# Full-width products, overwritten at once, in front of the compressed scores and of the combination products of an attention layer

## The chip, the cores and the metric

One core of a Trainium2 chip runs one launch of the kernel. The metric is the device time of that launch in microseconds (us). All work is in float32. Matrix products run on TensorE (PE in the profile, with its weight loads as PEld), elementwise work on VectorE (DVE), ScalarE (ACT) and GpSimd (POOL), and SyncE (SP) issues the DMAs. TensorE writes into PSUM, which has eight banks of 128 partitions by 512 float32 columns. The profile also lists the clock that TensorE was granted: 1.00 stands for 2.4 GHz, 0.50 for 1.2 GHz.

## What is computed

Two layers over 512 tokens of width 1024. Each layer is a gated feed-forward network, a mixer, and a second feed-forward network, each with a norm before and after and a residual. The mixer of the first layer is sparse attention (the change lies there), that of the second layer is a recurrent RWKV-7 block. Of the attention, cut to what matters:

```
q, kc, vc, ks, vs, kw, vw, gl = split(u @ w_in)        # 16 query heads, 4 key/value heads
k_cmp = compress(kc); v_cmp = compress(vc)             # 31 compressed blocks of 32 tokens
s_c = q . k_cmp - slope * dist;  p_c = masked softmax; o_c = p_c . v_cmp
s_s = q . ks    - slope * dist;  p_s = masked softmax; o_s = p_s . vs      # selected branch
s_w = q . kw    - slope * dist;  p_w = masked softmax; o_w = p_w . vw      # window branch
out = (g0 * o_c + g1 * o_s + g2 * o_w) @ w_out
```

With 512 tokens all eight selection blocks are taken, so the selected branch and the window branch both are causal attention over all tokens, with keys and values of their own.

## The kernel before

`nsa` first projects the compressed keys and values and the first queries, and then goes through the four key/value groups `g`, each with four query heads `u`, and in each group through the four blocks `b` of 128 queries. For one block `scores` makes q.k for both branches into a bank of PSUM (lines 654 and 655, key parts `kh` and `kl`), VectorE adds the bias and takes the minimum (line 657), ScalarE takes the exponential (line 659). `outputs` turns the weights with transposes (line 671), splits them into two parts (lines 200 and 201), and multiplies them with the values (lines 676 and 678).

Beside these rounds runs a list of other work, `fill`, whose steps are put between theirs by numbers (`BASE`, `PACE`): the remaining projections through `mm3` (line 195, three products for one), and for each group `compressed(g)` and `turned(g)`. `compressed(g)` writes 16 narrow products, one for each block and head (line 601: 128 rows of weights `q`, 32 moving columns of `kcmp`), into the columns of one PSUM bank; VectorE and ScalarE make the softmax from it (lines 604 to 619). The profile shows two records for each of these products. `turned(g)` transposes the result (line 626).

`combine(g-1)` runs inside the first block of group g, and `combine(3)` at the end. It transposes the reciprocal sums (line 698) and then, for each of two pairs of heads `j`, makes the compressed branch's output `cm` (line 706: `vbd`, `pcts`, 64 rows, 512 columns, two records each), spreads the gates with `pick` (line 714), and adds the three branches on VectorE and GpSimd (lines 715 to 717). Behind the attention comes the projection by `w_out` (line 195, `part` and `whi`).

The order of instructions on each engine is not the order of the code: a scheduler with a model of the times sorts them. A scheduler's choice can thus move other work when instructions are added. `xh` is the normed input of the attention, in 8 tiles of 128 features by 512 tokens; it is in place before the attention begins and stays until after it.

Of the kernel before, what the change touches and what calls it, by code (L numbers as in the profile page):

```python
# [16 lines left out]
P = 128  # L17
# [5 lines left out]
NB = S // P  # L23
# [46 lines left out]
class Net:  # L70
# [367 lines left out]
    def nsa(self, xh, xl):  # L438
        nc, io = self.nc, self.io
# [155 lines left out]

        def compressed(g):
            gv = gates[:, :, 12 * g:12 * g + 12].rearrange("p b (u r) -> p b r u", r=3)
            sb = self.bank().rearrange("p (b u n) -> p b u n", b=NB, u=4)
            for b in range(NB):
                for u in range(4):  # L600
                    nc.tensor.matmul(sb[:, b, u, :], qs[4 * g + u][:, b * P:b * P + P].bitcast(F32), kcmp[:, g, :],
                                     start=True, stop=True)
            sc = self.small([P, NB, 4, 32], "scc", 2)
            for u in range(4):
                nc.vector.scalar_tensor_tensor(sc[:, :, u, :], distc, slopes[4 * g + u], sb[:, :, u, :],
                                               op0=OP.mult, op1=OP.add)

            def wide(t):
                return t.rearrange("p b (u o) -> p b u o", o=1).to_broadcast([P, NB, 4, 32])
            mn = self.small([P, NB, 4], "mnc", 2)  # L610
            nc.vector.tensor_reduce(mn, sc, axis=AX.X, op=OP.min)
            nc.vector.tensor_tensor(sc, sc, wide(mn), op=OP.subtract)
            nc.scalar.activation(sc, sc, AF.Exp, scale=-1.0)
            al = self.small([P, NB, 4], "alc", 2)
            nc.vector.tensor_reduce(al, sc, axis=AX.X, op=OP.add)
            nc.vector.reciprocal(al, al)
            nc.vector.tensor_tensor(al, al, gv[:, :, 0, :], op=OP.mult)
            nc.vector.tensor_tensor(sc, sc, wide(al), op=OP.mult)
            nc.vector.tensor_tensor(sc[:, 0], sc[:, 0], maskc, op=OP.mult)
            scs[g] = sc  # L620
            yield
# [42 lines left out]
        def outputs(g, b, brs):  # L664
            tb = slice(b * P, b * P + P)
            for br in brs:
                ac = self.bank("ac")
                for k in range(b + 1):
                    tp = self.bank("pt")
                    for u in range(4):  # L670
                        nc.tensor.transpose(tp[:, u * P:u * P + P], ps[g, b, br, u][:, k * P:k * P + P], self.ident)
                    pt = [self.small([P, S], "pt", NPT, F32R) for _ in range(2)]
                    self.split(tp, *pt)

                    w = vt[k][:, br, g]
                    nc.tensor.matmul(ac, w.rearrange("p i d -> p (i d)"), pt[0], start=k == 0, stop=k == b,
                                     skip_group_check=True)
                    nc.tensor.matmul(ac[0:64], w[:, 0], pt[1], start=False, stop=k == b, skip_group_check=True)
                    yield
                if b + br == 0:  # L680
                    if g:
                        yield from combine(g - 1)
                    os[g] = self.small([P, 2, 2, S], "o", 1)
                hv = self.small([64, S], "hv", 1)
                nc.scalar.activation(hv, ac[64:128], AF.Copy)
                for e in range(2):
                    x, y = [t.rearrange("p (j e t) -> p j e t", j=2, e=2)[:, :, e, :] for t in (ac[0:64], hv)]
                    nc.vector.tensor_add(os[g][64 * e:64 * e + 64, br, :, tb], x, y)

        def combine(g):  # L690
            al, o = als[g % 2], os[g]
            av = al[:, :, 0:8].rearrange("p b (r u) -> p b r u", r=2)
            gv = gates[:, :, 12 * g:12 * g + 12].rearrange("p b (u r) -> p b r u", r=3)
            nc.vector.reciprocal(av, sums[g])
            nc.vector.tensor_tensor(av, av, gv[:, :, 1:3, :], op=OP.mult)
            tp = self.bank("pt")
            for b in range(NB):
                nc.tensor.transpose(tp[0:32, b * P:b * P + P], al[:, b, :], self.ident)
            at = self.small([64, S], "at", 1, F32R)
            nc.scalar.activation(at[0:32], tp[0:32], AF.Copy)  # L700
            nc.vector.tensor_sub(at[32:64], tp[0:32], at[0:32].bitcast(F32))
            yield
            for j in range(2):
                cm = self.bank("pt")
                rows = slice(64 * j, 64 * j + 64)
                nc.tensor.matmul(cm, vbd[g][rows, :], pcts[g][rows, :], start=True, stop=True)
                if len(opair) == KT // 2 and g >= G // 2:

                    t = self.act.tile([P, KT, S], F32, tag="xl", name="xl")
                    opair.extend(t[:, i, :] for i in range(KT // 2))  # L710
                y = opair[2 * g + j]
                for br, dst in ((0, y), (1, o[:, 1, j])):
                    bc = self.bank("sc")
                    nc.tensor.matmul(bc, pick[:, 2 * br + j, :], at, start=True, stop=True)
                    nc.vector.tensor_mul(dst, o[:, br, j], bc)
                nc.vector.tensor_add(y, y, cm)
                nc.gpsimd.tensor_add(y, y, o[:, 1, j])
                yield
# [5 lines left out]
        def all_of(g):  # L724
            for _ in g:
# [8 lines left out]

        bias, sums, ps, os = {}, {}, {}, {}
        fill = Fill(vproj(), gproj(), compressed(0), qproj(2), turned(0), qproj(3), compressed(1), kproj(1, 0), turned(1),
                    kproj(1, 1), qproj(4), qproj(5), compressed(2), qproj(6), turned(2), qproj(7), compressed(3), turned(3))
        rounds = [(g, b, items, brs) for g in range(G) for b in range(NB) for items, brs in ITEMS[b]]
        all_of(scores(*rounds[0][0:3]))
        n = 0  # L740
        for r, (g, b, _, brs) in enumerate(rounds):
            ahead, m = iter(()), 0
            if r + 1 < len(rounds):
                f, c, items, _ = rounds[r + 1]
                if f > g:
# [3 lines left out]
                    n = 0  # L749
# [11 lines left out]
            all_of(ahead)  # L761
        fill.until(1000)
        all_of(combine(G - 1))
        self.kinds = KINDS
        self.pop(2)
# [832 lines left out]
```

## Time and profile before

| | us |
|---|---|
| median of 3 runs (2302.13 to 2304.86) | 2302.98 |
| the profiled execution | 2306.49 |
| its span, first to last instruction | 2304.6 |
| PE busy in the span | 2190.6 (95%) |
| DVE busy | 1527.2 (66%) |
| ACT busy | 1159.3 (50%) |
| mean granted TensorE clock | 0.963 |

The attention's rounds lie from about 447 to 730 us of the span. The page gives the whole execution; what a stage is worth is read from windows cut out of it, where the busy time of each engine stands beside the granted clock. In the timeline a matmul's start is exact and its end is modelled, with neighbours overlapping; the price of one in a row is therefore the time from its start to the start of the next.

### The profile page before, as it was taken

How to read it: one execution, taken by the hardware profiler on the slowest of the kernel's cores; microseconds unless marked ns; L12 is line 12 of the kernel's file. 1: busy time of each engine (PE TensorE's matmuls, PEld its weight loads, DVE VectorE, ACT ScalarE, POOL GpSimd, SP SyncE). 2: the span in 40 equal slices, each digit the busy share in tenths (PEclk: the TensorE clock that was granted, in tenths of full speed). 3: DMA queues.
4: the chain of work that ended last, by engine and by line, in shares of the span. 5: the costliest groups of instructions: out<-in, count | busy, mean ns of one | idle time of the engine just before them, and what ended most of it. 6: DMA issues, size and time to landing. Idle time of an engine off the chain costs nothing.

```text
span 2304.6 us, 38449 instructions
## 1 busy us (share of the span) xinstructions
PE 2190.6 (95%) x15398; PEld 1921.0 (83%) x15398; DVE 1527.2 (66%) x2447; ACT 1159.3 (50%) x2282; POOL 363.9 (16%) x372
## 2 busy tenths in 40 slices
PE   7999999999999999999999999988699989899998
PEld 7999888877666889998799998866587867899987
DVE  8888625346777688872588874386663556888733
ACT  5555514465665455552445554286333754555532
POOL 4000004023100310000130000012493423100000
PEclk9999999999989999999999999999798989999999
DMA  4333333211001323333323333232443124333331
GB/s 174 101 104 111 101 95 109 83 46 46 29 1 65 101 83 110 107 94 102 110 83 100 103 101 108 85 104 92 75 114 122 47 83 162 94 109 99 96 107 67
DMA packets 93283, 214.33 MB, mean 93 GB/s; under 512 B 40752, under 2 KB 41392, under 8 KB 93104
## 3 DMA queue, kind: packets, MB, share of 16 engines
q1 hardware_dynamic: 93104, 211.88, 29.6%
q8 instruction: 121, 1.98, 0.4%
q14 instruction: 58, 0.48, 0.1%
HBM read 196.84 MB, written 15.01 MB: 92 GB/s over the span
## 4 chain that ended last, share of the span: by engine, by line
issue 29%; PE 24%; DVE 5%; POOL 4%; ACT 3%; DMA 1%; SPq 0%; DVEq 0%; POOLq 0%; ACTq 0%
PE p L195 19%; POOL two L1045 1%; POOL tmpi L1043 1%; PE p L1154 1%; ACT junk L218 1%; POOL sp L347 1%; PE p L1178 0%; DVE slot L201 0%; PE p L1170 0%; DVE xl L201 0%; DVE h L261 0%; PE p L972 0%; PE p L862 0%; PE p L1206 0%; PE p L1199 0%
## 5 line engine op out<-in xcount | busy, mean ns | idle before, releaser
L195 PE MATMUL p<-xh,whi 128*128 128x256 f32 (+1 forms) x1640 | 479.4, 296 | 18.3 <-ACT xh L200 8.4
L195 PE MATMUL p<-xl,whi 128*128 128x256 f32 (+1 forms) x1640 | 477.4, 294 | 3.4 <-DVE xl L201 3.4
L195 PE MATMUL p<-xh,wlo 128*128 128x256 f32 (+1 forms) x1640 | 457.9, 294 | 1.4 <-DVE wlo L201 1.4
L174 DVE TENSOR_TENSOR wlo<-raw,whi 128x1024 fp32r<-128x1024 f32 x150 | 190.2, 1269 | 316.7 <-ACT whi L170 316.7
L195 PE MATMUL p<-whi,slot 128*128 128x512 f32 x1280 | 395.1, 389 | 0.0
L195 PE MATMUL p<-slot,whi 128*128 128x256 f32 x1920 | 361.1, 284 | 12.5 <-issue 6.0
L170 ACT ACTIVATE whi<-raw 128x1024 fp32r<-128x1024 f32 x166 | 174.8, 1056 | 339.8 <-PE p L195 314.9
L195 PEld LDWEIGHTS p<-xh,whi 128*128 128x128 f32 x1640 | 319.1, 195 | 29.2 <-ACT xh L200 9.8
L195 PEld LDWEIGHTS p<-xl,whi 128*128 128x128 f32 x1640 | 320.2, 195 | 9.0 <-DVE xl L201 4.7
L195 PEld LDWEIGHTS p<-slot,whi 128*128 128x128 f32 x1920 | 303.4, 193 | 14.9 <-issue 6.2
L195 PEld LDWEIGHTS p<-xh,wlo 128*128 128x128 f32 x1640 | 309.5, 195 | 6.8 <-DVE wlo L201 1.6
L200 ACT ACTIVATE whi<-xn 128x1024 fp32r<-128x1024 f32 (+1 forms) x240 | 220.0, 917 | 184.7 <-PE p L195 133.8
L201 DVE TENSOR_TENSOR wlo<-xn,whi 128x1024 fp32r<-128x1024 f32 (+1 forms) x240 | 255.8, 1067 | 50.1 <-ACT whi L200 47.0
L195 PEld LDWEIGHTS p<-whi,slot 128*128 128x128 f32 x1280 | 240.0, 188 | 49.7
L195 PE MATMUL p<-slot,wlo 128*128 128x256 f32 x960 | 270.1, 284 | 0.0
L195 PE MATMUL p<-wlo,slot 128*128 128x512 f32 x640 | 249.0, 389 | 0.0
L222 POOL TENSOR_TENSOR rstd<-rstd,mhalf 128x1 f32<-128x1 f32 x48 | 30.1, 628 | 1348.0 <-DVE rstd L221 1347.2
L195 PEld LDWEIGHTS p<-slot,wlo 128*128 128x128 f32 x960 | 184.5, 193 | 0.0
L391 ACT ACTIVATE sp<-p 128x256 f32<-128x256 f32 x320 | 121.2, 379 | 112.6 <-PE p L195 112.6
L195 PEld LDWEIGHTS p<-wlo,slot 128*128 128x128 f32 x640 | 120.1, 188 | 24.9
L195 PE MATMUL p<-big,whi 128*128 128x512 f32 (+1 forms) x288 | 94.9, 412 | 12.0 <-ACT big L839 11.2
L200 ACT ACTIVATE whi<-raw 128x1024 fp32r<-128x1024 f32 x80 | 84.1, 1051 | 40.1 <-PE p L195 40.1
(321 smaller groups left out, 3754.1 us busy)
## 6 DMA issues: line engine op xcount, KB each, us to landing
raw<-in_wpack SPq DMA_DIRECT2D x252, 512.0 KB, 3.6
xn<-in_wpack SPq DMA_DIRECT2D x80, 512.0 KB, 3.5
hpark<-h SPq DMA_DIRECT2D x8, 512.0 KB, 2.7
h<-hpark SPq DMA_DIRECT2D x8, 512.0 KB, 4.7
h<-in_x SPq DMA_DIRECT2D x4, 512.0 KB, 7.1
gpost<-in_ffn_norm_post SPq DMA_DIRECT2D x4, 512.0 KB, 6.6
md<-tb SPq DMA_DIRECT2D x8, 256.0 KB, 2.8
td<-two SPq DMA_DIRECT2D x4, 512.0 KB, 2.8
```

The source lines that it names most:

```text
L170: self.last_hi = nc.scalar.activation(hi, raw, AF.Copy)
L174: (eng or nc.vector).tensor_sub(lo, raw, hi.bitcast(F32))
L195: m = self.nc.tensor.matmul(out, lhs[a], rhs[b], start=start and i == 0, stop=stop and i == 2, skip_group_check=more)
L200: i = self.nc.scalar.activation(hi, src, AF.Copy)
L201: return i, (eng or self.nc.vector).tensor_sub(lo, src, hi.bitcast(F32))
L218: nc.scalar.activation(self.junk(), src[q], AF.Square, scale=1.0 / (half * math.sqrt(D)), accum_out=ss[:, q:q + 1])
L222: nc.gpsimd.tensor_tensor(r[:, 1:2], r[:, 0:1], self.mhalf[:, 0:1], op=OP.pow)
L347: nc.gpsimd.tensor_sub(t4, q(xh, 1, 0, b), t2)
L391: copy = lambda dst, bank: nc.scalar.activation(dst, bank[:, 0:H], AF.Copy)
L1043: nc.gpsimd.tensor_tensor(t, ms[:, j, j + 1:32].rearrange("p (i o) -> p i o", o=1).to_broadcast([P, n, m]), T[:, j:j + 1, 0:m].to_broadcas ...
L1045: nc.gpsimd.tensor_tensor(T[:, j + 1:32, 0:m], T[:, j + 1:32, 0:m], t, op=OP.subtract)
L1154: nc.tensor.matmul(gb[e][:, j * P:j * P + P], B[own[e], j, c, :], A[own[e], j, c, :], start=True, stop=True)
```

## The change

In `compressed(g)`, ahead of the four narrow products of each block `b`, one product of `xh` with itself goes into the same bank, over all columns from that block on (512, 384, 256 and 128 columns for b = 0 to 3). In `combine(g)`, ahead of the product into `cm`, two products of 512 columns go into the same bank, for each `j`. All have 128 rows of weights and are written with start=True; the products behind them overwrite what they wrote, so no value of the output depends on them. They come to 16 products in `compressed` and 16 in `combine`, 20 of them with 512 columns.

```diff
         def compressed(g):
             gv = gates[:, :, 12 * g:12 * g + 12].rearrange("p b (u r) -> p b r u", r=3)
-            sb = self.bank().rearrange("p (b u n) -> p b u n", b=NB, u=4)
+            bank = self.bank()
+            sb = bank.rearrange("p (b u n) -> p b u n", b=NB, u=4)
             for b in range(NB):
+
+                nc.tensor.matmul(bank[:, b * P:], xh[:, 0, 0:P], xh[:, 0, b * P:], start=True, stop=True)
                 for u in range(4):
                     nc.tensor.matmul(sb[:, b, u, :], qs[4 * g + u][:, b * P:b * P + P].bitcast(F32), kcmp[:, g, :],
                                      start=True, stop=True)
...
             for j in range(2):
                 cm = self.bank("pt")
                 rows = slice(64 * j, 64 * j + 64)
+                for _ in range(2):
+                    nc.tensor.matmul(cm, xh[:, 0, 0:P], xh[:, 0, :], start=True, stop=True)
                 nc.tensor.matmul(cm, vbd[g][rows, :], pcts[g][rows, :], start=True, stop=True)
```

In the changed file the new products stand on lines 602 and 710; line 601 becomes 604, 654 becomes 657, 655 becomes 658, 671 becomes 674, 676 becomes 679, 678 becomes 681, 698 becomes 701, 706 becomes 711 and 714 becomes 719.

TensorE, the compressed scores of the first group (bank p_5203), before:

```order
L592 MATMUL p_5179<-ident,at 128x64 x4
L601 MATMUL p_5203<-kcmp,q 128x32 x8
L654 MATMUL p_4996<-kh,q 128x384
L655 MATMUL p_4996<-kl,q 128x384
L601 MATMUL p_5203<-kcmp,q 128x32 x2
```

and after:

```order
L592 MATMUL p_5179<-ident,at 128x64 x4
L602 MATMUL p_5203<-xh 128x512
L604 MATMUL p_5203<-kcmp,q 128x32 x4
L602 MATMUL p_5203<-xh 128x384
L604 MATMUL p_5203<-kcmp,q 128x32 x3
L657 MATMUL p_4996<-kh,q 128x384
```

Two of the four new products stand inside what was a row of eight narrow ones; everything ahead of this place on TensorE is unmoved.

TensorE, the compressed scores of the second group (p_5453, after p_5457), before:

```order
L601 MATMUL p_5453<-kcmp,q 128x32 x2
L676 MATMUL p_5122<-pt,vt_3970 128x512
L654 MATMUL p_5408<-kh,q 128x256
L655 MATMUL p_5408<-kl,q 128x256
L601 MATMUL p_5453<-kcmp,q 128x32
L678 MATMUL p_5122<-pt,vt_3970 64x512
```

```order
L601 MATMUL p_5453<-kcmp,q 128x32 x10
L671 MATMUL p_5430<-ident,sp 128x128
L601 MATMUL p_5453<-kcmp,q 128x32 x3
```

and after, where the first combination product of the first group has moved ahead of them:

```order
L710 MATMUL p_5543<-xh 128x512 x2
L711 MATMUL p_5543<-scc,vbd_3981 128x512
L657 MATMUL p_5412<-kh,q 128x256
L658 MATMUL p_5412<-kl,q 128x256
L604 MATMUL p_5457<-kcmp,q 128x32
L602 MATMUL p_5457<-xh 128x384
L604 MATMUL p_5457<-kcmp,q 128x32 x4
L602 MATMUL p_5457<-xh 128x256
L604 MATMUL p_5457<-kcmp,q 128x32 x4
L602 MATMUL p_5457<-xh 128x128
L604 MATMUL p_5457<-kcmp,q 128x32 x3
```

The narrow ones still stand close together, now with three new products among them and two ahead.

TensorE, the compressed scores of the fourth group (p_7081, after p_7105) and the combination of the second (`vbd_3982`), before:

```order
L706 MATMUL p_6251<-scc,vbd_3982 128x512
L654 MATMUL p_6240<-kh,q 128x256
L655 MATMUL p_6240<-kl,q 128x256
L714 MATMUL p_6253<-at,pick 128x512
L671 MATMUL p_6277<-ident,sp 128x128 x4
L601 MATMUL p_7081<-kcmp,q 128x32 x10
L706 MATMUL p_6261<-scc,vbd_3982 128x512
```

and after:

```order
L710 MATMUL p_6267<-xh 128x512 x2
L711 MATMUL p_6267<-scc,vbd_3982 128x512
L657 MATMUL p_6256<-kh,q 128x256
L658 MATMUL p_6256<-kl,q 128x256
L719 MATMUL p_6271<-at,pick 128x512
L674 MATMUL p_6297<-ident,sp 128x128 x4
L604 MATMUL p_7105<-kcmp,q 128x32
L602 MATMUL p_7105<-xh 128x384
L604 MATMUL p_7105<-kcmp,q 128x32 x4
L602 MATMUL p_7105<-xh 128x256
L604 MATMUL p_7105<-kcmp,q 128x32 x4
L710 MATMUL p_6279<-xh 128x512 x2
```

Here the row of ten narrow products is cut by two new ones and stands between two pairs of full width.

## Rows read from the trace of the kernel before

**Rows 1.** The page: engines (busy us, share, instructions) and granted clock in 40 slices.

```profile
PE 2190.6 (95%) x15398; PEld 1921.0 (83%) x15398; DVE 1527.2 (66%) x2447; ACT 1159.3 (50%) x2282; POOL 363.9 (16%) x372
PEclk9999999999989999999999999999798989999999
```

**Rows 2.** Stretches: start:end, length, busy PE, PEld, DVE, ACT, POOL, granted clock, DMA.

```profile
496.40:498.17 1.77, 1.77 (x18) 1.72 (x16) 1.65 (x5) 1.73 (x3) 0.00 (x0) 1.00 0.42 104
498.17:508.41 10.24, 10.24 (x35) 7.52 (x34) 3.18 (x8) 4.52 (x12) 0.00 (x0) 0.50 0.09 35
525.47:528.88 3.41, 3.41 (x10) 2.64 (x9) 3.13 (x9) 1.94 (x5) 2.98 (x2) 0.50 0.05 20
533.00:542.50 9.50, 9.50 (x68) 8.03 (x67) 7.01 (x24) 7.40 (x21) 2.38 (x1) 1.00 0.18 56
600.57:603.98 3.41, 3.41 (x10) 2.73 (x10) 2.40 (x7) 0.63 (x1) 0.00 (x0) 0.50 0.00 0
631.28:655.18 23.90, 23.90 (x71) 16.01 (x70) 15.57 (x40) 7.02 (x19) 2.54 (x2) 0.50 0.00 1
655.18:730.27 75.09, 72.05 (x324) 42.91 (x322) 63.38 (x172) 57.33 (x147) 5.54 (x4) 1.00 0.00 1
730.27:737.10 6.83, 6.05 (x13) 4.23 (x14) 6.83 (x10) 3.23 (x6) 2.94 (x2) 0.50 0.09 20
```

**Rows 3.** Timeline of TensorE at the narrow products of three groups: start, us, instruction.

```profile
496.45 2.09 PE L601 MATMUL p<-kcmp,q 128*128 128x32 f32 x16
498.35 0.67 PE L654 MATMUL p<-kh,q 128*128 128x384 f32 x1
...
538.44 2.42 PE L601 MATMUL p<-kcmp,q 128*128 128x32 f32 x20
540.70 0.31 PE L671 MATMUL p<-ident,sp 128*128 128x128 f32 x1
...
597.57 2.54 PE L601 MATMUL p<-kcmp,q 128*128 128x32 f32 x22
```

**Rows 4.** Timeline of TensorE: starts that follow one another, at full and half clock.

```profile
487.00 0.39 PE L195 MATMUL p<-xh,whi 128*128 128x512 f32 x1
487.23 0.39 PE L195 MATMUL p<-xl,whi 128*128 128x512 f32 x1
...
490.16 0.48 PE L195 MATMUL p<-xl,whi 128*128 128x512 f32 x1
490.48 0.34 PE L654 MATMUL p<-kh,q 128*128 128x384 f32 x1
...
622.83 0.28 PE L654 MATMUL p<-kh,q 128*128 128x256 f32 x1
623.04 0.38 PE L655 MATMUL p<-kl,q 64*128 64x256 f32 x1
...
735.09 0.63 PE L195 MATMUL p<-whi,part 128*128 128x512 f32 x1
735.51 0.63 PE L195 MATMUL p<-wlo,part 128*128 128x512 f32 x1
```

**Rows 5.** Timeline of TensorE in the longest stretch at half clock.

```profile
633.29 4.31 PE L601 MATMUL p<-kcmp,q 128*128 128x32 f32 x20
637.54 2.07 PE L706 MATMUL p<-scc,vbd 64*128 64x512 f32 x2
```

**Rows 6.** Timeline of VectorE there: one wait in brackets, with what ended it.

```profile
640.93 0.69 DVE L715 TENSOR_TENSOR o<-o,p 128x512 f32<-128x512 f32 x1 [5.42 <-PE p L714]
```

**Rows 7.** Timeline of TensorE at the attention's end, waits in brackets.

```profile
730.19 1.39 PE L714 MATMUL p<-at,pick 64*128 64x512 f32 x2 [1.29 <-DVE xl L715]
732.36 0.80 PE L195 MATMUL p<-whi,part 128*128 128x512 f32 x1 [0.78 <-ACT part L200]
```

## The prediction

> **What bounds the kernel now.** I read the page first [rows 1]: TensorE is busy for 95% of the span, and the row of granted clocks is below 9 in a few slices only. One of them lies in the attention (the slices are 57.6 us long, and the twelfth of the row covers most of 634 to 691 us). So I cut the attention into stretches by granted clock [rows 2]. The reader is to see two things there. First, in each of these stretches up to 655 us TensorE is busy from end to end (10.24 of 10.24, 9.50 of 9.50, 23.90 of 23.90), while VectorE, the next engine, has room: 15.57 of 23.90 in the longest, 63.38 of 75.09 behind it. The stage is bound by TensorE, and a microsecond more or less of work there is a microsecond of the span, as long as VectorE doesn't become the bound. Second, five stretches stand at 0.50, which is 1.2 instead of 2.4 GHz: 10.24, 3.41, 3.41, 23.90 and 6.83 us, together 47.8 us.
>
> Then I looked at what TensorE did before the clock fell. At 496.45 it ran 16 records of the narrow compressed scores in 2.09 us, and the clock was at half by 498.17; at 597.57 it ran 22 of them in 2.54 us, and the clock was at half by 600.57 [rows 2, 3]. TensorE never stopped in the first case (1.77 of 1.77 us), so the fall isn't made by a wait; what is special is that 32 columns leave the array little to do for each load of weights. It isn't strict: 20 records in 2.42 us at 538.44 left the clock at 1.00 through 542.50 [rows 2, 3]. The longest stretch holds 20 such records (4.31 us) and two combination products of 64 rows (2.07 us), both at the lower clock [rows 5].
>
> **What a stretch at half clock is worth.** The same 512-column product starts 0.23 us before its follower at full clock (487.00 to 487.23) and 0.42 us before it at half (735.09 to 735.51) [rows 4]. Work that takes 1 us at half takes 0.23/0.42 = 0.55 us at full, so 0.45 us comes back for each; with the narrower rows rounded in I take 0.47. All five stretches hold at most 47.8 x 0.47 = 22.5 us.
>
> **The added products.** 32 products, all on TensorE's path, with nothing to hide them but its few waits. A 512-column one costs 0.23 us if it flows into the next and 0.32 us if an instruction with another kind of weights follows (490.16 to 490.48) [rows 4]. The 16 of the combinations stand in pairs: 0.23 for the first and 0.32 for the second give 8 x 0.55 = 4.4 us; the bounds are 16 x 0.23 = 3.7 and 16 x 0.32 = 5.1 us. Those of the scores have 512, 384, 256 and 128 columns: by columns alone 0.23 x (1 + 0.75 + 0.5 + 0.25) = 0.58 us for a group. From above, 0.32 for the widest, no more than that for the next, 0.21 us for 256 columns by the product at 622.83 [rows 4], and the same for 128, give 1.06 us. I take 0.8, as the last two are near the lower end when the next load is short: 4 x 0.8 = 3.2 us, bounds 2.3 to 4.2. Together **7.6 us, bounds 6.0 to 9.3**; a product that falls into a stretch at half clock costs 0.42/0.23 times its share. They wait for nothing new: the bank is the one that the products behind them need anyway, and `xh` is long in place. Behind them on TensorE stand the scores and transposes of the round, for which VectorE and ScalarE wait. No transfer is added, and queues other than TensorE's see only the scheduler's shifts.
>
> **What comes back.** The first stretch (10.24 us) begins 1.7 us into a row of narrow products. Everything ahead of it on TensorE is unmoved, and now a 512- and a 384-column product stand in that row, so I expect it to go: 10.24 x 0.47 = 4.8 us, bounds 0 to 4.8. The second and third (3.41 us each) are worth 1.6 us each. The second stands at no added product, and its neighbours are only shifted; the third stands behind a row that is cut three times. I take one of the two, 1.6 us, bounds 0 to 3.2. The fourth (23.90 us) is the prize. By TensorE it is worth 23.90 x 0.47 = 11.2 us; but VectorE has 15.57 us of work inside it, so no more than 8.3 us can go from this stretch while VectorE keeps its work there, and part of VectorE's room is one wait of 5.42 us for TensorE [rows 6], which shrinks with it. The row before it is now cut by three products and flanked by two pairs. I take 7 us, bounds 0 to 8.3. VectorE's slack behind it (11.7 us of 75.09) is enough not to give that back. The fifth (6.83 us) stands where TensorE waits 1.29 us for VectorE and 0.78 us for ScalarE [rows 7] and VectorE is busy all the time [rows 2]; at full clock TensorE would mostly wait for the splits. I take 1 us, bounds 0 to 3.2. Against this stands a new fall: the second group's narrow products, which went through at full clock, stand closer now than before. A fall there costs as much as one or two of the short stretches, 1.6 to 3.2 us; I set 1.6.
>
> Sum: 7.6 - (4.8 + 1.6 + 7 + 1 - 1.6) = 7.6 - 12.8 = **-5.2 us**. The span of the profiled execution would go from 2304.6 to 2299.4 us, its time from 2306.49 to 2301.3. The median of the runs lies 3.5 us under the profiled time, and the same difference gives 2302.98 - 5.2 = **2297.8 us**. What lies behind the attention is unchanged in work; the clock falls there too, at places that shift by a few microseconds, and the runs of before differ by 2.7 us among themselves, so I allow 1.4 us to either side.
>
> A rule that speaks against the change. The row shows TensorE busy for all of the 1.77 us ahead of the first fall, and at work without a break in the narrow products [rows 2, 3]. The Trainium skill, page "TensorE: Matmul & The Clock Gate", section "Why this matters for your kernels", advises against gaps in which TensorE idles between bursts of matmuls, as the cause of throughput drops in mid-kernel. By that rule the added products, which fill no gap, would leave every fall where it is, and the sum would be the bare cost; by the rows the fall came without a gap. The trace speaks against the rule here, and I keep it as the last rival.
>
> **The rivals.** *VectorE takes over.* The clock is held, but in the fourth stretch TensorE then waits for VectorE's bias, split and combination work: 3 us come back there instead of 7, 4.8 at the first stretch, 1 elsewhere, less 1.6 for the new fall. That is 7.2 against 7.6: 2303.4 us. For it speaks 15.57 us of work in a stretch that should shrink to some 15; against it that VectorE's idle time there was spent waiting for TensorE.
>
> *The clock falls all the same (slower).* The narrow products still stand in rows; three wider ones among sixteen may be too few, and then the clock falls at the second group's scores as well and stays low from the fourth group's scores on. One mechanism decides, whether the fourth group's scores pass at full clock: if they don't, the stretch of 23.90 us stays, with its 7 added products at double price. Price: 7.6 + 1.5 for these + 3.2 for the second group - 4.8 for the first = 7.5 us: 2310.5. For it: at half clock the rounds of the fourth group kept the clock low for the whole of 631.28 to 655.18, so one fall there costs many microseconds [rows 2]. Against it: the same kind of row passed at 538.44 with no help at all.
>
> *The clock doesn't follow the width of products.* If only idle time counts, nothing comes back and the bare 7.6 us are added: 2310.6. Against it speaks the first fall, as said.
>
> **How the numbers follow.** The forecast has 0.50 (its own range 2288 to 2301, from gains near all upper bounds and the lower cost to a fourth stretch half gone), VectorE's rival 0.18, the falling clock 0.25, the last 0.07. A measurement of this kernel tells about 0.2%, or 4.6 us, from no change, so faster means under 2298.4. Of the forecast's 0.50 I put 0.41 under that line and 0.09 above, since the sum lies close to it: faster 0.41. Within: 0.09 + 0.18 + 0.03 of the falling clock = 0.30. Slower: 0.22 + 0.07 = 0.29. The range 2288 to 2311 leaves out the best of the forecast (0.05) and what lies above the two slow rivals' prices (0.13).
>
> **What would show it.** In the changed profile the stretch from 496 to 508 at 1.00 would show the first step right, and one at 0.50 there wrong. The added lines should have 32 records and start 0.2 to 0.35 us ahead of their followers. The stretch in which the second combination and the fourth scores stand should be at 1.00 and under 20 us long; there VectorE's share tells whether the gain stopped at VectorE (near all of it busy, TensorE with waits) or went through. A new stretch at 0.50 near 540 us is the fall that I priced at 1.6. The prediction is wrong if the total at 0.50 between 447 and 740 us stays above 40 us, or if it falls under 15 us without the time following.

## The result and the profile after

The changed kernel takes 2315.39 us (median of 5 runs, 2314.66 to 2322.24), the kernel before 2302.13 us beside it (5 runs, 2298.86 to 2304.86). The ratio is 1.0065 with an interval of 1.0047 to 1.0083: slower by 0.65%. The forecast was 2297.8 us with a range up to 2311, so both the sign and the range were wrong.

The page of after, granted clock (for [rows 1]): the dark slice in the attention is gone.

```profile
PEclk9999999999999999999999999999798989999999
```

Stretches of after (for [rows 2]): start:end, length, busy PE, PEld, DVE, ACT, POOL, granted clock, DMA.

```profile
497.50:510.00 12.50, 12.50 (x76) 9.84 (x76) 8.57 (x24) 9.73 (x21) 0.50 (x1) 1.00 0.13 43
544.38:547.79 3.41, 3.41 (x10) 2.73 (x10) 2.99 (x9) 0.98 (x4) 0.00 (x0) 0.50 0.00 0
602.41:605.82 3.41, 3.41 (x10) 2.54 (x9) 2.65 (x7) 1.19 (x2) 0.00 (x0) 0.50 0.00 0
646.78:653.61 6.83, 6.83 (x19) 4.05 (x17) 5.31 (x17) 4.93 (x13) 0.00 (x0) 0.50 0.00 0
694.57:697.98 3.41, 3.41 (x11) 2.35 (x11) 2.49 (x8) 1.98 (x7) 0.00 (x0) 0.50 0.03 7
732.12:735.53 3.41, 3.41 (x9) 2.65 (x8) 3.41 (x5) 1.76 (x4) 1.66 (x1) 0.50 0.00 0
```

The five at 0.50 come to 20.5 us, where before had 47.8 [rows 2]. The first stretch is gone as forecast, the new one near 544 is there, the fourth is 6.83 instead of 23.90 us. The attention of this execution is faster: instructions behind it, which stood 1.6 us late at 480 us, stand 1.6 us early at 771, so 3.2 us were won. All of the loss comes later: 2.7 us late at 1138, 5.1 at 1480, 9.0 at the end. That is the first thing to explain; the second is whether the 3.2 us are real, as this is one execution.

The added products cost what they were priced at. TensorE's timeline in after shows a pair and what follows it, and one at the scores:

```profile
538.12 0.62 PE L710 MATMUL p<-xh 128*128 128x512 f32 x2
538.68 1.12 PE L711 MATMUL p<-scc,vbd 64*128 64x512 f32 x2
...
540.60 0.42 PE L602 MATMUL p<-xh 128*128 128x384 f32 x1
540.87 0.30 PE L604 MATMUL p<-kcmp,q 128*128 128x32 f32 x2
```

A pair takes 0.56 us (538.12 to 538.68; 0.55 in the prediction), the product of 384 columns 0.27 (540.60 to 540.87).

### The profile page after: what moved, and what is told of

Read it like the earlier page. It is cut to its first block, busy times and chain, and to the rows that moved or that the text cites. A ratio compares the mean times of both kernels' runs of the same rounds, so it can differ in the third digit from the quotient of the medians.

```text
span 2313.6 us, 38514 instructions
## 1 busy us (share of the span) xinstructions
PE 2191.3 (95%) x15430; PEld 1923.1 (83%) x15430; DVE 1526.3 (66%) x2447; ACT 1159.3 (50%) x2282; POOL 359.5 (16%) x372
## 4 chain that ended last, share of the span: by engine, by line
issue 29%; PE 24%; DVE 5%; POOL 4%; ACT 3%; DMA 1%; SPq 0%; DVEq 0%; POOLq 0%; ACTq 0%
PE p L195 19%; POOL tmpi L1048 1%; POOL two L1050 1%; PE p L1159 1%; ACT junk L218 1%; POOL sp L347 1%; DVE slot L201 1%; PE p L1183 0%; DVE wlo L174 0%; PE p L1175 0%; DVE h L261 0%; DVE xl L201 0%; PE p L977 0%; PE p L867 0%; POOL rstd L222 0%
## 5 line engine op out<-in xcount | busy, mean ns | idle before, releaser
L195 PE MATMUL p<-slot,whi 128*128 128x256 f32 x1920 | 363.8, 286 | 12.6 <-issue 6.0
L195 PE MATMUL p<-big,whi 128*128 128x512 f32 (+1 forms) x288 | 94.7, 411 | 12.0 <-ACT big L844 11.3
```

The source lines that it names most:

```text
L195: m = self.nc.tensor.matmul(out, lhs[a], rhs[b], start=start and i == 0, stop=stop and i == 2, skip_group_check=more)
```

## The experiments

**How the parts were separated.** The scheduler had also reordered instructions behind the attention, in the two feed-forward networks and in the RWKV block, on VectorE and TensorE above all. The experiments write the order down: a table `ORDER` holds each engine's instructions in the order of one of the two built kernels, and an edge that waits for nothing ties each to the one ahead of it. The added products are left out of the table and stay where their banks put them. Every kernel computes all of the reference. The tables are packed text; the cuts below name them by what they hold, and from the third run on they are shown against a run with a table, not against the two built kernels.

```diff
+ORDER = {...}
+ADDED = []
...
+        row = [int(x) for x in d + np.arange(len(d)) if x >= MARK.get(e, 0)]
+        for a, b in zip(row, row[1:]):
+            tc.add_manual_dep(mine[b], mine[a].name, nosync, reason="placed")
...
         build(tc, out, io)
+        placed(tc, nc)
```

`MARK` is the end of the attention on each engine; without the condition on it the whole program is tied.

**Products, with the order behind kept.** The changed kernel, with everything behind the attention in the order of before.

```diff
-nc.tensor.matmul(cm, xh[:, 0, 0:P], xh[:, 0, :], start=True, stop=True)
+ADDED.append(nc.tensor.matmul(cm, xh[:, 0, 0:P], xh[:, 0, :], start=True, stop=True).ins)
```

(and the same at the scores)

> The changed kernel (all 32 products, the attention in the changed order), but everything traced behind the attention is held, engine by engine, in the order that the kernel before has there. Theory O (order): the attention itself gains about 5 us (the two traces run from +1.6 us before it to -3.3 us at 798 us of the span) and the loss comes from the scheduler's other order of the second feed-forward network and the stages behind it; then this run is about 2302 - 5 = 2297 us, and the stretch 798 to 817 us loses nothing against before. Theory C (clock): the loss comes from where the stages behind happen to meet the falls of the clock, whatever their order; then this run stays at 2308 to 2322 us.

Measured 2309.02 us, ratio 1.0032 (1.0020 to 1.0044). Half of the loss is gone with the order behind; the time lies in theory C's range all the same.

**Products, with the whole order kept.** As above, without the condition on `MARK`.

> All 32 products, but every other instruction of every engine in the order of the kernel before, the attention's too. Theory O: the products alone give what they cost and bring in the attention, and nothing behind it changes: 2295 to 2300 us. Theory C: 2305 to 2320 us, as the changed kernel. If the attention's gain came from its new order and not from the products, this run shows the bare cost, about 2302 + 7 = 2309 us, with the stretches at 1.2 GHz of before still there.

Measured 2311.67 us, ratio 1.0048 (1.0032 to 1.0064). Keeping the attention's order as well takes nothing more away; the intervals overlap.

**The changed order behind, without products.** The kernel before, with the table of after behind the attention.

```diff
-ORDER = {... of before}
+ORDER = {... of after, its 32 products taken out}
```

> No products; the attention as in the kernel before, but everything traced behind it in the changed kernel's order. Theory O: the loss behind the attention comes along without the products: about 2302 + 11 to 14 = 2313 to 2316 us, and 5 to 6 us of it are lost by 817 us of the span. Theory C: within 3 us of 2302 us.

Measured 2312.22 us, ratio 1.0043 (1.0024 to 1.0062). No product is added here, and more than half of the loss is there. With the first run: 0.32% + 0.43% = 0.75%, against 0.65% measured for both.

**The changed order everywhere, without products.** As above, without the condition on `MARK`.

> No products, every engine in the changed kernel's order, the attention's too. Theory O: the loss behind (11 to 14 us) without the products' 7.6 us and without what they bring: if the products hold the clock up, the attention keeps 40 us or more at 1.2 GHz here and the time is 2311 to 2318 us; if the attention's new order held the clock up, the attention has 20 us at 1.2 GHz and the time is 2303 to 2309 us. Theory C: 2298 to 2308 us.

Measured 2312.34 us, ratio 1.0054 (1.0037 to 1.0071): the same as the order behind alone, within the intervals.

**The kernel before once more**, as a control of the comparison.

> The kernel before, unchanged, with a profile of its own. Theory P (the falls are drawn anew in each execution): the stretches at 1.2 GHz in the attention differ from those of the first profile, where they came to 47.8 us, though every instruction is in the same place; the time agrees with before to 2 us in the median. Theory F (the falls are fixed by the program): the same five stretches, within half a microsecond of where they stood.

Measured 2302.38 us, ratio 1.0007 (0.9991 to 1.0024). Its profile speaks for theory P: with every instruction in its place the first fall in the attention had 6.83 instead of 10.24 us, and there was one of 3.41 us at 537.81 that the first profile lacks.

**The changed order in the feed-forward networks alone**, and **in the RWKV block alone.** The table of before, with the positions of the one part taken from after:

```diff
-ORDER = {... of before}
+ORDER = {... of before; of after between the attention and RWKV}
```

```diff
-ORDER = {... of before}
+ORDER = {... of before; of after from RWKV on}
```

> No products, the attention in the order of before; only the two feed-forward networks behind the attention stand in the changed kernel's order (293 of TensorE's matmuls, 44 of VectorE's and 21 of ScalarE's instructions stand at another place), the recurrent block as before. The order behind cost 10 to 12 us with both parts. If the feed-forward part makes it: 2307 to 2312 us, and a loss by 817 us of the span; if the recurrent block makes it: 2298 to 2303 us.

> No products; only the recurrent block stands in the changed kernel's order (72 matmuls, 9 instructions of VectorE, 11 of ScalarE, 6 DMA issues at another place). If it makes the loss behind the attention: 2306 to 2312 us, with more time at 1.2 GHz between 1500 and 1990 us than before; if the feed-forward part does: 2298 to 2303 us. If any small change of order costs the same, because the kernel before holds an order that suits the clock by selection, both parts alone cost 5 us or more.

Measured 2306.9 us, ratio 1.0022 (1.0008 to 1.0036), and 2309.84 us, ratio 1.0032 (1.0015 to 1.0048). Both cost, where each expectation had named one. By the account further below it is 4 and 7 us, near the 5 us and more that the last expectation gives for any small change of order.

For the feed-forward network the trace shows how. VectorE's order at one place, before and then after (`xl` on line 201 are splits that TensorE waits for, line 340 sums of activations, lines 375 to 379 sums of weights that come by DMA):

```
L201 xl x2 | L234 xn | L340 sp | L375 xn | L378 xn | L341 sp | L376 xn
L201 xl    | L234 xn | L375 xn | L378 xn | L201 xl | L376 xn | L340 sp
```

VectorE's timeline there, before (start, us, instruction, wait in brackets):

```profile
795.77 1.78 DVE L340 TENSOR_TENSOR sp<-xh 128x512 f32<-128x512 f32 x1
797.48 0.68 DVE L375 TENSOR_TENSOR xn<-xn 128x512 f32<-128x512 f32 x1
```

and in after:

```profile
797.32 0.69 DVE L375 TENSOR_TENSOR xn<-xn 128x512 f32<-128x512 f32 x1 [3.67 <-DMA xn<-in_wpack]
```

In before a split and the 1.78 us of line 340 run while the transfer lands, and line 375 waits for nothing. In after line 375 comes first, waits 3.67 us for the transfer, and the second split stands behind it. TensorE's timeline in after shows the wait that follows:

```profile
803.96 0.58 PE L195 MATMUL p<-xl,whi 128*128 128x256 f32 x1 [3.52 <-DVE xl L201]
```

In the run with this part's order alone VectorE and TensorE show the same two waits:

```profile
797.07 0.69 DVE L375 TENSOR_TENSOR xn<-xn 128x512 f32<-128x512 f32 x1 [1.33 <-DMA xn<-in_wpack]
```

```profile
803.72 0.39 PE L195 MATMUL p<-xl,whi 128*128 128x256 f32 x1 [1.15 <-DVE xl L201]
```

All eight profiled executions with this order, the five of the changed kernel among them, have TensorE's wait (1.1 to 3.5 us). The five of the kernel before have none there, and the others with the order of before have 0.63 us at most. In after the clock falls at the end of this wait. The 30 us of this place in before, and two waits in them that left the clock at 1.00:

```profile
800.00:830.00 30.00, 24.46 (x195) 23.36 (x194) 29.60 (x40) 15.43 (x30) 14.49 (x7) 1.00 0.20 59
```

```profile
816.72 0.39 PE L195 MATMUL p<-xh,whi 128*128 128x256 f32 x1 [1.57 <-ACT sp L322]
820.83 0.51 PE L195 MATMUL p<-slot,whi 128*128 128x256 f32 x2 [2.43 <-ACT sp L391]
```

After:

```profile
800.00:830.00 30.00, 22.82 (x159) 22.02 (x158) 29.71 (x39) 13.59 (x25) 15.38 (x8) 0.89 0.12 36
```

VectorE bounds this place, not TensorE: it is busy for 29.60 and 29.71 of the 30 us, and TensorE for 24.46 and 22.82. So what VectorE waits for the transfer is lost. In after its line 341 starts at 811.89 instead of 809.63, though the instructions at 771 us stood 1.6 us early: 3.9 of the 4.3 us that this network loses. The fall of the clock costs little here. With RWKV's order alone, where this place has the order of before, a fall of 3.41 us left the network's time unchanged to 0.1 us:

```profile
820.16:823.57 3.41, 3.41 (x18) 3.41 (x18) 3.41 (x7) 0.78 (x3) 1.60 (x1) 0.50 0.11 7
```

With the feed-forward order alone the clock holds through the wait of 1.15 us, but VectorE is 2.0 us behind (its line 341 starts at 811.67 instead of 809.63; 0.5 us of it stood already at 771), and the two waits that follow, hardly longer than before's, come with a fall of 10.24 us. By 830 us the loss has grown from 1.5 to 3.0 us:

```profile
818.75 0.38 PE L195 MATMUL p<-xh,whi 128*128 128x256 f32 x1 [1.93 <-ACT sp L322]
...
823.42 1.37 PE L195 MATMUL p<-slot,whi 128*128 128x256 f32 x3 [2.46 <-ACT slot L200]
```

```profile
819.67:829.91 10.24, 7.78 (x35) 7.20 (x34) 10.00 (x11) 4.46 (x9) 6.03 (x4) 0.50 0.17 51
```

In the RWKV block, in the run with its order alone, I found longer waits of TensorE for VectorE (line 1154: 3.2 us against 2.2; line 1104: 2.6 against 1.7) and longer falls around 1710 and 1766 us (10.2 and 17.1 us, against 6.8 and 13.7), but did not follow them to one instruction; the run with the networks' order alone, with RWKV's order of before, had 1.8 and 2.2 us at these lines. The fall near 1710 goes with the order: it has 6.8 us in all twelve executions with the order of before there, and 10.2 or 13.6 us in seven of the eight with the changed one. The fall near 1766 doesn't: it has 10.2 to 20.5 us in the five executions of before.

**The products of the scores alone**, all else in the order of before (shown against the run with the whole order kept, as in the next one).

```diff
-                for _ in range(2):
-                    ADDED.append(nc.tensor.matmul(cm, xh[:, 0, 0:P], xh[:, 0, :], start=True, stop=True).ins)
```

> Only the 16 products in front of the compressed scores, every other instruction of every engine in the order of before. All 32 in that order cost 9 to 12 us. By bare price (3.2 us) and with nothing brought in: 2303 us. If they hold the clock up at the scores: 2296 to 2300 us. If they bring in less than they cost and add falls elsewhere: 2304 to 2308 us.

Measured 2312.79 us, ratio 1.0046 (1.0027 to 1.0064), above all that was expected. The execution profiled is one of the slowest of its twelve (2322.16 us). In it three products among the fourth group's scores don't hold the clock:

```profile
632.78:666.91 34.13, 34.13 (x97) 21.93 (x96) 20.44 (x52) 12.29 (x32) 2.55 (x2) 0.50 0.00 1
```

Nor did the first fall go, though a 512- and a 384-column product stand in the first group's row here as in after. It had 6.83 us from 503.07 on, and the same length in the run with all 32 products and the whole order kept:

```profile
500.29:507.12 6.83, 6.83 (x24) 5.25 (x24) 2.01 (x6) 2.03 (x6) 0.00 (x0) 0.50 0.00 0
```

**The products of the combinations alone.**

```diff
-                ADDED.append(nc.tensor.matmul(bank[:, b * P:], xh[:, 0, 0:P], xh[:, 0, b * P:], start=True, stop=True).ins)
```

> The 16 full-width products of the combinations alone; every other instruction of each engine stands where it stood before the change. Theory now (the products cost their own time, and the spots at 1.2 GHz are moved about but not taken away): the 16 cost their 4.4 us by the prediction's own prices, and the fourth group's long stretch (23.9 us before) is shorter, since two pairs stand right beside it; total near +2 to +6 us, 2302 to 2306 us. The products of the scores alone gave +0.46%, all 32 in the same order +0.48%. If the two sets add up, this one is within 0.1% of before. Rival (any added product costs by shifting what lies behind): +0.4% here as well, 2309 us or more, with as long a stretch at the fourth group as before.

Measured 2310.84 us, ratio 1.0033 (1.0014 to 1.0051). The fourth stretch was 6.82 us in the one execution profiled, as my theory had it, and the time above 2306 all the same, as the rival had it.

**Products only at the longest stretch**, first in front of both products of the second group's combination and at the fourth group's scores, then in front of one product alone.

```diff
+                if g == 3:
+                    ADDED.append(nc.tensor.matmul(bank[:, b * P:], xh[:, 0, 0:P], xh[:, 0, b * P:], start=True, stop=True).ins)
...
-                for _ in range(2):
+                for _ in range(4 if g == 1 else 0):
```

```diff
-                for _ in range(2):
+                for _ in range(8 if g == 1 and j == 1 else 0):
```

> Only products around the longest stretch at 1.2 GHz: four of 512 columns in front of each of the two products of the second group's combination, and the four of the fourth group's scores; 12 in all, every other instruction where it stood before the change. Cost by the prices at full clock: 8 x 0.23 + 2 x 0.09 + 0.8 = 2.8 us. Theory that dense work ahead of the fourth group's scores holds the clock there: the stretch of 23.9 us (13.7 to 34.1 in the runs so far) falls below 10 us, 7 to 11 us come back, and the time goes to 2292 to 2297 us, faster than both kernels. Rival (the long stretch comes from the narrow products themselves and from the rounds behind them, whatever stands ahead): 20 us or more remain there, and the time is 2303 us or more.

> As the run before, but with no products at the scores and with all eight of 512 columns in front of one product, the second pair of heads of the second group's combination, which stands right behind the fourth group's narrow scores; cost 8 x 0.23 = 1.8 us at full clock, 3.4 at half. Theory that a low clock ends as soon as a few us of full-width products run: the fall at the fourth group's scores still begins near 632 us, and ends behind these products, so the stretch is 7 to 14 us long; time 2294 to 2299 us. Rival (the clock stays low through the rounds behind in any case): a stretch of 20 us or more and 2302 us or more.

Measured 2304.25 us, ratio 1.0015 (0.9999 to 1.0031), and 2306.86 us, ratio 1.0018 (1.0001 to 1.0035). Again the long stretch is short, here in the first of the two:

```profile
644.32:651.14 6.82, 6.17 (x16) 3.60 (x15) 5.59 (x18) 3.54 (x12) 0.00 (x0) 0.50 0.00 0
```

and again the time doesn't follow. In the second the fall began at 641.23 us, behind the eight products and not ahead of them near 632 as expected. Neither beats the kernel before; no version here does.

**Both kernels again, with more profiles.** Nothing is edited.

> The changed kernel once more, beside the same runs of before as the other three. If products (+0.32% with the order behind kept) and the changed order behind (+0.43%) add up: +0.65 to +0.75%, 2315 to 2317 us. The profiled execution of the changed kernel had 20.5 us at 1.2 GHz within the attention, the same attention with the order behind kept had 44.4: if these falls vary from execution to execution, this one lies between 20 and 45; if the changed kernel really loses fewer, it lies within a stretch of 20.5.

Measured 2321.61 us, ratio 1.0069 (1.0048 to 1.0089): the share is the sum expected, the median lies 4.6 us above 2317.

> One more profiled execution of the kernel before. Time at 1.2 GHz between 447 and 745 us: five profiled executions with this attention had 47.8, 44.4, 30.7, 47.8 and 44.4 us. If the products take falls away, this one stands at 40 to 48 us; if the executions differ among themselves as widely as the kernels do, one of the three stands at 35 us or less.

> One more profiled execution of the changed kernel. Time at 1.2 GHz between 447 and 745 us: 20.5 and 30.7 us so far, 44.4 with the same attention and the order behind it kept. If the products take falls away: 20 to 31 us. If executions differ as widely as kernels: one of the three at 40 us or more. Behind the attention a fall of 3.4 to 10.2 us between 800 and 825 us in every one of them, by the changed order of the feed-forward net there.

> As the first look at the kernel before: 40 to 48 us at 1.2 GHz in the attention, or 35 and less in one of the three.

> As the first look at the changed kernel: 20 to 31 us at 1.2 GHz in the attention, or 40 and more in one of the three; the fall between 800 and 825 us in each.

> Third look at the kernel before. If the products take falls away: 40 to 48 us at 1.2 GHz in the attention, as in most of the profiled executions so far; if executions differ as widely as kernels, 35 or less in one of the three looks.

> Third look at the changed kernel: 20 to 31 us at 1.2 GHz in the attention if the products take falls away, 40 or more in one of the three looks if executions differ as widely as kernels; a fall between 800 and 825 us in each.

Measured, before: 2300.38, 2311.58 and 2298.96 us; after: 2326.25, 2316.23 and 2315.41 us. One kernel's attention differs from execution to execution: two of these three of before are under 35 us, one of after is over 40. The fourth stretch in the first of these executions of before, where [rows 2] had 23.90 us:

```profile
635.61:649.26 13.65, 13.65 (x36) 8.11 (x36) 11.00 (x31) 6.08 (x16) 2.56 (x2) 0.50 0.00 0
```

and in the first of these of after, where the profile above had 6.83, with the last of the fourth group's narrow products ahead of it:

```profile
638.08 0.41 PE L604 MATMUL p<-kcmp,q 128*128 128x32 f32 x2
```

```profile
640.50:674.63 34.13, 34.13 (x88) 20.33 (x87) 20.25 (x56) 18.51 (x47) 1.28 (x1) 0.50 0.00 0
```

So the fourth group's narrow products pass at full clock here, and the fall comes behind them, in the rounds of scores, transposes and value products. It is so in all five executions of after (the last narrow product starts between 637.95 and 640.74 us, the fall between 640.25 and 646.78), and in two of the five of before, the ones with 13.65 us. In the other three of before the fall begins 1 to 2 us ahead of the long row of narrow products (631.28 and 633.29 us in the first [rows 2, 5]).

All profiled executions of the two kernels, in us. The middle columns say how much later the same instructions end than in the profiled execution of before, gained or lost within each part.

| | attention at 1.2 GHz | of it fourth | to 480 | attention to 771 | first network to 1138 | second to 1480 | RWKV and the rest | span |
|---|---|---|---|---|---|---|---|---|
| before | 47.8 | 23.9 | 0 | 0 | 0 | 0 | 0 | 2304.6 |
| before again | 44.4 | 23.9 | -0.1 | -1.4 | 0.0 | 0.1 | 0.0 | 2303.2 |
| before, third | 30.7 | 13.7 | 1.6 | -7.7 | 0.0 | 0.1 | -0.1 | 2298.5 |
| before, fourth | 51.2 | 23.9 | -0.8 | 1.7 | 0.0 | 0.2 | 4.0 | 2309.6 |
| before, fifth | 30.7 | 13.7 | -0.2 | -7.8 | 0.0 | 1.0 | -0.6 | 2297.1 |
| **mean** | 41.0 | 19.8 | 0.1 | -3.0 | 0.0 | 0.3 | 0.7 | 2302.6 |
| after | 20.5 | 6.8 | 1.6 | -3.2 | 4.3 | 2.5 | 3.9 | 2313.6 |
| after again | 30.7 | 20.5 | 1.5 | 0.0 | 2.9 | 2.7 | 7.7 | 2319.4 |
| after, third | 44.4 | 34.1 | -0.1 | 5.8 | 3.8 | 2.7 | 7.7 | 2324.5 |
| after, fourth | 30.7 | 20.5 | 1.0 | -0.6 | 3.7 | 2.2 | 3.5 | 2314.5 |
| after, fifth | 27.3 | 13.7 | -0.3 | -1.8 | 3.6 | -0.1 | 7.6 | 2313.6 |
| **mean** | 30.7 | 19.1 | 0.7 | 0.0 | 3.7 | 2.0 | 6.1 | 2317.1 |

The difference of the means is 14.5 us: 0.7 ahead of the attention, 3.1 in it, 3.6 in the first network, 1.7 in the second, 5.4 from RWKV on. With five executions each the attention's 3.1 is uncertain by about 2.5, RWKV's 5.4 by 1.3, the first network's 3.6 by 0.2 us (one standard error each), so the 3.1 isn't clear of nothing. The second network's 1.7 isn't the order's: it is reordered too, and two of the three runs with its changed order and no products lose nothing there (-0.1 us; the third 1.0). It goes with the clock: 13.6 us at 1.2 GHz between 1138 and 1480 us in the four executions of after that lose 2.2 to 2.7 us, 6.8 in the fifth and in four of before. Why the clock is low for longer there stays open.

**All runs in one account.** Each run lists its span and mean granted clock, so its time at 1.2 GHz is 2 x (1 - clock) x span. Two executions of before that differ by 17.1 us of it in the attention (47.8 and 30.7) differ by 7.7 us there, 0.45 for one. Means against the 83 runs of before beside the experiments (span 2300.5, clock 0.9654, so 159 us at 1.2 GHz):

| | at 1.2 GHz | products, priced | price + 0.45 x change | measured |
|---|---|---|---|---|
| 32 products, order behind kept | 154 | 7.6 | 5.4 | 6.0 |
| 32 products, order kept | 169 | 7.6 | 12.1 | 9.0 |
| order behind alone | 178 | 0 | 8.6 | 9.1 |
| whole order, no products | 180 | 0 | 9.5 | 10.8 |
| order of the networks alone | 172 | 0 | 5.9 | 4.2 |
| order of RWKV alone | 170 | 0 | 5.0 | 7.1 |
| products of the scores | 177 | 3.2 | 11.3 | 10.5 |
| products of the combinations | 172 | 4.4 | 10.3 | 9.6 |
| 12 products at the long stretch | 160 | 2.8 | 3.3 | 3.8 |
| 8 products before one | 166 | 1.8 | 5.0 | 4.5 |
| changed kernel, first 5 runs | 170 | 7.6 | 12.6 | 15.3 |
| changed kernel, other 6 | 179 | 7.6 | 16.6 | 17.4 |

The account closes to about 3 us. In ten of twelve rows the time at 1.2 GHz rose by 7 us or more, and in none did it fall by more than 6. It is a rough balance and shows no cause: the 0.45 comes from a stage that TensorE bounds, and over the whole program the 83 runs of before give 0.35 for one. With 0.35, five of the six rows with the changed order behind come out 2.5 to 3.9 us short, as they would if that order cost something besides the clock, like VectorE's wait.

## Why the prediction was wrong, point by point

**Where the difference lies.** The forecast was -5.2 us, the difference between the means of the profiled executions is +14.5. Of these 19.7 us, 10.7 lie behind the attention, which the sum put at nothing; 8.2 are gain that was counted on and didn't come; 0.7 stood ahead of the attention.

**"What lies behind the attention is unchanged in work", with 1.4 us to either side.** This is the step that took the time out of the range. The work is unchanged, its order isn't, and the order behind costs 9 us by itself (0.43%). The reordered rows could have been read ahead of the run, as those in the attention were; I read only the part that the change touched. A plain sign stood there: an instruction that needs a DMA had moved ahead of a split that TensorE waits for. The rule that I set aside, of the Trainium skill ("TensorE: Matmul & The Clock Gate", section "Why this matters for your kernels"), warns of idle gaps of TensorE between bursts of matmuls. For the first network the trace agrees with it: a wait of 3.52 us, and the clock at 0.89 in the 30 us around it, 1.00 before. But most of that network's loss is VectorE's own wait, not the clock. Nor does the rule decide alone: waits of 1.57 and 2.43 us left before's clock at 1.00 and waits of 1.93 and 2.46 us didn't leave it there in the run with the networks' order, and the fourth group's fall in before came with TensorE busy from end to end [rows 2].

**The added cost, 7.6 us.** Right within its bounds. Pairs take 0.56 us where 0.55 was priced, and the attention's means give 3.1 + 0.45 x (41.0 - 30.7) = 7.7 us. In the order of before the one profiled execution with all 32 products lost 1.8 us in the attention at 37.6 us at 1.2 GHz, which gives 6.3 us against the means of before by the same sum.

**What a stretch at half clock is worth, 0.47.** Right in the attention: 0.45. By the table, the time lost in the attention less 0.45 for each us at 1.2 GHz is -21.3 to -21.6 in all five executions of before, and -12.4 to -14.4 in those of after.

**What comes back, 12.8 us.** This step failed too, and made the sign wrong: by the means the attention alone is 3.1 us slower. 4.6 us came back, from 10.3 us fewer at 1.2 GHz on the average, and with a standard error of 6 us that isn't clear of nothing. The first stretch did go, in all five executions of after, but it is 6.8 us in four of the five of before and 10.2 only in the one that I read, so it is worth 3.1 to 4.6 us. It wasn't the products alone: with them in the order of before it stood with 6.83 us in both executions profiled, and the changed order without them had 3.41 us in its one. The fall at the second group, which I counted as new, has 6.8 us in four of five of after, but stood in four of five of before too, near 538 us with 3.4 us (once 6.8); the execution that I read was the one without. The fourth stretch, worth 7 in the sum, is 19.8 us on the average before and 19.1 after: nothing came back. I called the narrow products the row before it; by the rows they start at 633.29 us, 2 us behind the fall at 631.28 [rows 2, 5]. In after they passed at full clock each time, as I had hoped, and the fall came behind them. I took the 47.8 us of one execution for the kernel's; two of its five executions had 30.7.

**The profile of after would have misled.** It met most of the signs that I had set (496 to 508 at 1.00, the fourth stretch under 20 us, a new fall near 540) and read alone says that the attention worked. It is the lowest of five.

**The rivals.** In the attention the second one came nearest: the clock fell at the second group's scores in all five, and in four stayed low for 13.7 us and more, though from behind the fourth group's scores and not from them on: the one mechanism that it named, whether these pass at full clock, didn't decide. Its price of 7.5 us was above the 3.1 measured there. The third, that width doesn't matter and the bare cost is added, isn't excluded: the gain of 4.6 us isn't clear of nothing. VectorE did not take over: in the 34.13 us stretch it is busy for 20.25 and TensorE for all. No rival had the order behind, and the range's upper end, 2311, was that of a kernel whose attention alone gets slower.

**What stays open.** In the three kernels that add products at the combinations and not at every group's scores the fourth stretch was 6.8 us in the one execution profiled of each, against 13.7 to 27.3 us in the eight with the attention of before, and their mean time at 1.2 GHz was still not under that of before. Where it lies in the executions without a profile isn't known; from 1480 to 1990 us, where RWKV lies, the time at 1.2 GHz varies by 24 us between executions that have the order of before there (81.9 to 105.8 us). Whether any other order of RWKV would cost as much wasn't run; that a changed order need not cost is shown by the second network only.

## What to carry to other kernels

Instructions added in one place change what a scheduler does with all that follows: compare the built orders to the end of the program, and look for an instruction that waits for a transfer and has moved ahead of one that the bound engine waits for. Where the clock moves from execution to execution, profile each kernel several times before sizing a stretch, and separate order from work by writing the order down. See which engine bounds each stage before a fall of TensorE's clock is priced there. Filling products are paid for in full, and here nothing reliable came back.

## What the runs showed of the hardware

- One program's time at 1.2 GHz differs between executions by about 40 us: 83 runs of before had 142 to 185 us of it by their mean clocks and went from 2294.65 to 2313.25 us; the profiled ones had 30.7 to 51.2 us in the attention alone.
- In the attention, which TensorE bounds, 1 us at 1.2 GHz cost 0.45 us in all five executions of before. In the first network, where VectorE was busy for 29.60 of 30 us, a fall of 3.41 us cost nothing.
- The falls keep their places roughly: the fourth group's began between 630.0 and 635.6 us in every execution of before. Their lengths don't: 23.9 us where it began ahead of the long row of narrow products, 13.65 where it began behind, with TensorE busy from end to end in both.
- Wide products among narrow ones did not keep the clock up: with three wider products among the fourth group's sixteen narrow ones the clock was low for 34.13 us in one execution, with the scores' products alone, against 13.65 to 27.31 us in the eight with the attention of before.
